# Sums of squares along the rows of x on ScalarE for groups two to eight, with a rewritten order of the preparation steps

## The chip, the core and the metric

The kernel runs on one core of a Trainium2 chip. The core has five engines with instruction queues of their own: TensorE (PE in the profile, its weight loads PEld), VectorE (DVE), ScalarE (ACT), GpSimd (POOL) and SyncE (SP, which here only issues transfers). Each works through its own instructions in program order and waits on semaphores for the others. Transfers run on 16 DMA engines. The metric is device time in microseconds (us) of one execution; of several executions the median counts.

## The reference: one hybrid attention and retention layer

The input is x (2048 tokens by 1024, float32), 256 context tokens `ctx`, a conditioning vector c with its twin `c_ctx`, and the weights of one layer. The part that matters here is the beginning: each token is normalised by its root mean square, scaled and shifted by vectors that come from c through the matrix `w_ada`, and projected by `w_in`.

```python
def _rmsnorm(x, g):
    xf = x.astype(jnp.float32)
    xf = xf * lax.rsqrt(jnp.mean(xf * xf, axis=-1, keepdims=True) + EPS)
    return (xf * g.astype(jnp.float32)).astype(x.dtype)
...
mod = jax.nn.silu(c) @ w_ada[i] + b_ada[i]
mod_c = jax.nn.silu(c_ctx) @ w_ada[i] + b_ada[i]
...
h_lat = _rmsnorm(x, norm_g[i]) * (1.0 + scale) + shift
h_ctx = _rmsnorm(ctx, norm_g[i]) * (1.0 + scale_c) + shift_c
...
y_lat, y_ctx = _mixer(h_lat, h_ctx, w_in[i], ...)
x = x + gate * y_lat
return _rmsnorm(x, final_norm_g)
```

`_mixer` projects h to eight blocks of columns, runs neighbourhood attention on four of them and two-way retention on the other four, and projects the result back. All of that stays as it is.

## The kernel before

**Groups.** The 2304 tokens are handled as nine groups of 256: groups 0 to 7 are x, group 8 is the context. The first stage makes h for each group and, while doing so, already projects it: block b (0 to 4) holds groups 2b and 2b+1, and `window(b)` runs 32 steps of three matmuls for it (four result tiles, `units`, of eight steps each). Products are made in pieces of a high and a low part, so h and the weights exist as `hi` and `lo` tiles. A step of block b has the number 32b + n, and `PLAN` names after which step each piece of preparation is issued. It is a table written out by hand; `run_acts` takes its entries in order. No scheduler changes it: what stands earlier in the program stands earlier in the queue of its engine.

**The pieces for group i.**
- `x`: the transposed group (features on partitions, tokens along the row) is loaded from `xT` (`load_x`, L182).
- `sq`: its squares and their partial sums over features (`squares`, L194). ScalarE squares two halves, and POOL and DVE add up the pieces into one 128x256 tile.
- `cs`: four small matmuls against a column of ones add over the partitions (`colsum`, L205), so that PSUM holds one sum per token.
- `rs`: DVE scales it and adds epsilon (L214), POOL raises it to the power -1/2 (L215), DVE copies it along a row (L220).
- `sp`: a matmul against the identity (`spread`, L222) turns it round, so that the factors lie along the row in PSUM.
- `mu`: DVE multiplies the group by the factors, half u at a time (L241).
- `ab`: scale and shift (`prep_ab`, L267), part on DVE, part on ScalarE; for groups 0 and 1 `p` does this per block of 128 features k together with the split into hi and lo (`prep_first`, L255).
- `hl`: ScalarE writes the hi part (L279), and POOL or DVE the lo part (L283).

**The vectors of c.** They come from four rows u of `w_ada`: `s` splits a piece, `m` multiplies (L311), `ar` copies the row out of PSUM (`ada_row`, L316), `af` turns it round and adds the bias (`ada_fin`, L321). Features k = 2u and 2u+1 need row u.

**What else runs there.** Every finished unit is evicted by `u_k` (L380): ScalarE casts it to the hi part (L383), DVE takes the lo part (L384), and SP stores both to `kS` in DRAM. The tile `o` for this has two buffers, so the third eviction waits until the first store has landed. `spill_step` (L249) stores h to `hS` in DRAM, one half group at every second step. The tiles named `st` (four of 512 KB) hold two groups of weights at first, then the squares, at last the context and weights again.

**Queues.** All loads and these stores are issued on SP in program order; an SP instruction that waits for data holds back every later one. `LOADS` is the list that SP issues first.

Of the kernel before, what the change touches and what calls it, by code (L numbers as in the profile page):

```python
# [9 lines left out]
F32 = mybir.dt.float32  # L10
BF16 = mybir.dt.bfloat16
F32R = mybir.dt.float32r
AF = mybir.ActivationFunctionType
# [5 lines left out]
P = 128  # L19
# [19 lines left out]
PLAN = [  # L39
# [19 lines left out]
]  # L59
SPL = [9, 0, 1, 0]  # L60
ALO = [0, 5, 9, 4]
# [21 lines left out]
def hybrid_kernel(ctx: ExitStack, tc: tile.TileContext, a: dict, out: bass.AP):  # L83
    nc = tc.nc
# [45 lines left out]
    KH = KC // 2  # L130
    env = dict(pp=pool(psx, "pp", 6, space=PSUM), st=pool(sx, "st", 4, side="right"), queue=nc.sync)

    def ptile(p=None):
        return (p or env["pp"]).tile([P, 512], F32, name="mm")
# [56 lines left out]

    sqs, rms, rbs, prs = {}, {}, {}, {}

    def squares(i):  # L194
        sqs[i] = []
        for u in range(2):
            sq = xsq[i][u] if i < 2 else env["st"].tile([P, KH, 256], F32, name="st")
            nc.scalar.activation(sq, raw[i][u], AF.Square)
            eng = (nc.gpsimd, nc.vector)[u]
            eng.tensor_tensor(sq[:, 0:2, :], sq[:, 0:2, :], sq[:, 2:4, :], ALU.add)  # L200
            eng.tensor_tensor(sq[:, 0, :], sq[:, 0, :], sq[:, 1, :], ALU.add)
            sqs[i].append(sq)
        nc.vector.tensor_tensor(sqs[i][0][:, 0, :], sqs[i][0][:, 0, :], sqs[i][1][:, 0, :], ALU.add)

    def colsum(*ii):  # L205
        pm = ptile(None if ii[0] < 4 else psm)
        for j, i in enumerate(ii):
            for t in range(2):
                nc.tensor.matmul(pm[:, 2 * j + t:2 * j + t + 1], sqs[i][0][:, 0, t * P:(t + 1) * P], one, start=True, stop=True)
            rms[i] = pm[:, 2 * j:2 * j + 2]  # L210

    def rstd(i):
        r = env["st"].tile([P, 2], F32, name="rs", bufs=4)
        nc.vector.tensor_scalar(r, rms[i], 1.0 / D, EPS, ALU.mult, ALU.add)  # L214
        nc.gpsimd.tensor_tensor(r, r, mhalf[:, 0:2], ALU.pow)  # L215
        rbs[i] = r

    def spread_copy(i):
        rbs[i, 1] = env["st"].tile([P, 2, P], F32, name="t0", bufs=2)
        nc.vector.tensor_copy(rbs[i, 1], rbs[i].unsqueeze(2).to_broadcast([P, 2, P]))  # L220
# [95 lines left out]
    def ada_row(u):  # L316
        rows[u] = op.tile([P, 2, 512], F32, name="o")[:, 0, :]
        n = 4 if SPL[u] else 2
        (nc.scalar.copy, nc.vector.tensor_copy)[u % 2](rows[u][0:n, :], aps[u][0:n, :])

    def ada_fin(u):  # L321
        pm, n = ptile(psm), 4 if SPL[u] else 2
# [141 lines left out]
    lds = dict(a=ada_load, x=load_x, c=small, w=lambda g: wr.append(w_raw(512 + 256 * g)))  # L464
    for name, *args in LOADS:
        lds[name](*args)
    acts = dict(sq=squares, cs=lambda *i: colsum(*i), rs=lambda i: (rstd(i), spread_copy(i)), sp=lambda *i: spread(*i),
                mu=lambda i, u: spread_mul(i, (u,)), ab=prep_ab, hl=prep_hl, blk=alloc_blk, x=load_x, w=lambda: wr.append(w_raw(2560)),
                w2=lambda: load_w(), s=ada_split, m=ada_mm, ar=ada_row, af=ada_fin, p=prep_first,
                ws=lambda g: w01.append(w_split(wr[g], lo=WSL[g])))  # L470
# [1151 lines left out]
```

## Time and profile before

| | |
|---|---|
| median of 3 runs | 1360.26 us (1356.26, 1360.26, 1361.77) |
| profiled execution, its own time | 1357.68 us |
| its span, from the first to the last instruction | 1355.7 us |
| mean granted TensorE clock | 0.996 |
| matmul instructions in the profile | 8236 |
| bytes moved by DMA | 287.25 MB |

Times inside the kernel are counted from the start of the span. A row of the timeline gives start, duration, engine, line, operation, written and read tiles, shape, a count and, in brackets, the idle time of the engine before it and what ended it. Durations of consecutive matmuls overlap, so the pace of TensorE is read from the distance of their starts. The stage that this document is about takes the first 165 us or so.

### The profile page before, as it was taken

To read this page: it belongs to the slowest core of one execution; us is meant where nothing else is said; L and a number is where in the kernel's file an instruction comes from. 1 tells how busy PE (TensorE), PEld (TensorE's weight loads), DVE (VectorE), ACT (ScalarE), POOL (GpSimd) and SP (SyncE) were. 2 spreads that over 40 slices of the span, in tenths; PEclk is the share of its full clock that TensorE was granted. 3 is DMA by queue.
4 is the path that set the end of the run, shared out by engine and by line. 5 is a ranking of instruction groups with operands and counts; after the bars stand their busy time and mean duration, and the time that the engine had idled before them with its cause. 6 is when DMAs were issued, how large, how long until landed. Compare 5 with 4: busy or idle time off the path is not lost.

```text
span 1355.7 us, 23094 instructions
## 1 busy us (share of the span) xinstructions
PE 1310.1 (97%) x8236; PEld 1146.9 (85%) x8236; DVE 828.3 (61%) x1444; ACT 606.5 (45%) x1259; POOL 579.9 (43%) x569
## 2 busy tenths in 40 slices
PE   6999999999999999999999999999999899999997
PEld 2477899887897788998999889889999789888886
DVE  5687366676766755377767777776654633445345
ACT  4454343343533344455555465556643244333432
POOL 4443101554034664445535474655523154544442
PEclk9999999999999999999999999999999999999999
DMA  9386788464867656978587886666528888555433
GB/s 363 135 279 231 259 313 215 164 210 147 326 182 230 216 203 213 265 210 211 148 225 207 226 224 206 195 181 193 163 90 291 278 290 279 159 163 171 163 121 129
DMA packets 172085, 287.25 MB, mean 212 GB/s; under 512 B 17345, under 2 KB 92225, under 8 KB 170690
## 3 DMA queue, kind: packets, MB, share of 16 engines
q1 hardware_dynamic: 139554, 228.35, 55.8%
q10 hardware_dynamic: 32416, 57.42, 11.8%
q8 instruction: 66, 1.08, 0.3%
q14 instruction: 49, 0.40, 0.1%
HBM read 194.48 MB, written 91.23 MB: 211 GB/s over the span
## 4 chain that ended last, share of the span: by engine, by line
PE 70%; DVE 9%; DMA 8%; POOL 4%; issue 4%; ACT 3%; SPq 1%; ACTq 0%; DVEq 0%; POOLq 0%
PE mm L374 17%; PE mm L671 12%; PE mm L1463 11%; PE mm L363 7%; PE sS L1025 4%; PE tr L1052 3%; PE po L1073 3%; PE mm L1187 2%; PE mm L311 2%; PE tr L1054 2%; PE po L1075 2%; DMA v<-rvS 1%; PE mm L1375 1%; POOL hlo L531 1%; PE mm L1374 1%
## 5 line engine op out<-in xcount | busy, mean ns | idle before, releaser
L374 PE MATMUL mm<-whi,hlo 128*128 128x256 f32 x832 | 228.6, 282 | 1.0 <-DMA hlo<-cS 1.0
L374 PE MATMUL mm<-whi,hhi 128*128 128x256 f32 x768 | 224.3, 292 | 0.0
L374 PE MATMUL mm<-wlo,hhi 128*128 128x256 f32 x768 | 216.8, 282 | 0.0
L1056 ACT CAST pt<-tr 128x640 fp32r<-128x640 f32 (+1 forms) x128 | 95.6, 747 | 160.4 <-PE tr L1054 157.8
L1062 DVE TENSOR_TENSOR pt<-tr,pt 128x640 fp32r<-128x640 f32 (+1 forms) x128 | 114.0, 890 | 78.4 <-ACT pt L1056 77.2
L374 PEld LDWEIGHTS mm<-whi,hlo 128*128 128x128 f32 x832 | 156.6, 191 | 1.4 <-DMA hlo<-cS 1.3
L1045 POOL TENSOR_SCALAR sp<-sp,stt 128x640 f32<-128x640 f32 (+2 forms) x128 | 103.1, 808 | 106.3 <-DVE stt L1044 75.7
L374 PEld LDWEIGHTS mm<-whi,hhi 128*128 128x128 f32 x768 | 146.3, 191 | 0.0
L374 PEld LDWEIGHTS mm<-wlo,hhi 128*128 128x128 f32 x768 | 146.1, 190 | 0.0
L1034 DVE CUSTOM_DVE_ANT_0 sp<-sS,nb 128x640 f32<-128x640 f32 (+2 forms) x128 | 105.6, 825 | 33.4 <-DMA nb<-in_rpb_t_dram 20.7
L1039 ACT ACTIVATE sp<-sp,stt 128x640 f32<-128x640 f32 (+2 forms) x128 | 107.4, 839 | 20.3 <-DVE stt L1034 19.1
L625 POOL TENSOR_TENSOR whi<-st,whi 128x512 fp32r<-128x512 f32 x48 | 62.8, 1330 | 107.7 <-ACT whi L624 107.7
L363 PE MATMUL mm<-hhi,whi 128*128 128x512 f32 x256 | 108.2, 423 | 0.0
L363 PE MATMUL mm<-hlo,whi 128*128 128x512 f32 x256 | 102.0, 399 | 6.0 <-DVE hlo L265 2.1
L1025 PE MATMUL sS<-k,q 128*128 128x256 f32 (+3 forms) x512 | 99.1, 315 | 5.1 <-DVE stt L1034 4.7
L363 PE MATMUL mm<-hhi,wlo 128*128 128x512 f32 x256 | 102.0, 398 | 0.3 <-DVE wlo L347 0.3
L671 PE MATMUL mm<-hhi,whi 128*128 128x512 f32 x336 | 98.1, 395 | 1.6 <-POOL whi L625 1.6
L1463 PE MATMUL mm<-wor,y 128*128 128x512 f32 x384 | 95.7, 398 | 1.1 <-DVE xt L1472 1.1
L1472 DVE TENSOR_TENSOR xt<-mm,xt 128x512 f32<-128x512 f32 x64 | 43.9, 687 | 82.6 <-PE mm L1463 82.5
L1025 PEld LDWEIGHTS sS<-k,q 128*128 128x128 f32 x512 | 82.8, 188 | 12.0 <-DVE stt L1034 8.2
L1463 PE MATMUL mm<-won,y 128*128 128x512 f32 x336 | 89.9, 406 | 0.0
L625 POOL TENSOR_TENSOR wlo<-st,wlo 128x512 fp32r<-128x512 f32 x36 | 53.1, 1476 | 75.8 <-ACT wlo L624 73.7
(258 smaller groups left out, 3051.5 us busy)
## 6 DMA issues: line engine op xcount, KB each, us to landing
st<-in_w_in_dram SPq DMA_DIRECT2D x64, 512.0 KB
q<-qS SPq DMA_DIRECT2D x64, 256.0 KB
hlo<-hS SPq DMA_DIRECT2D x20, 512.0 KB
k<-kS SPq DMA_DIRECT2D x16, 576.0 KB
kS<-o SPq DMA_DIRECT2D x16, 512.0 KB
vB<-o SPq DMA_DIRECT2D x64, 128.0 KB
qS<-o ACTq DMA_DIRECT2D x16, 512.0 KB
woS<-g ACTq DMA_DIRECT2D x32, 256.0 KB
```

Source lines behind the costliest of these rows:

```text
L363: nc.tensor.matmul(pm[:, :n], ww[:, k, cs], h[:, k, :], start=(k == 0 and i == 0), stop=(k == KC - 1 and i == 2))
L374: nc.tensor.matmul(pm[:, t * WG:(t + 1) * WG], h[:, k, o:o + P], ww[:, k, :], start=(k == 0 and i == 0), stop=(k == KC - 1 and i == 2))
L625: nc.gpsimd.tensor_tensor(t[:, 1], r, f(t)[:, 0], ALU.subtract)
L671: nc.tensor.matmul(pm, ww[:, k, :], hh[:, k, :], start=(k == 0 and i == 0), stop=(k == KH - 1 and i == 2))
L1025: nc.tensor.matmul(o, hd["q"][i][:, hl, j * P:(j + 1) * P], k, start=(hl == 0), stop=(hl == 1))
L1034: nc.vector.tensor_tensor_reduce(T["sp"][:, :n], T["s"], nbz[big][:, o:o + n], -1.0, 3e38, ALU.add, ALU.min, T["st"][:, 0:1])
L1039: nc.scalar.activation(sp[:, :n], sp[:, :n], AF.Exp, bias=st[:, 0:1], scale=-1.0, accum_out=st[:, 1:2])
L1045: nc.gpsimd.tensor_scalar(sp[:, :n], sp[:, :n], st[:, 2:3], 0.0, ALU.mult, ALU.add)
L1056: nc.scalar.copy(pt[:, :ng_ + 2, 0, :], tr[:, :ng_ + 2, :])
L1062: nc.vector.tensor_tensor(pt[:, :n, 1, :], tr[:, :n, :], f(pt)[:, :n, 0, :], ALU.subtract)
L1463: nc.tensor.matmul(pm, yy[:, k, :], ww[:, k, sl], start=(k == 0 and i == 0), stop=(k == 3 and i == 2))
L1472: nc.vector.tensor_tensor(xts[t][:, sl], pm, xts[t][:, sl], ALU.add)
```

## The change

Groups 2 to 8 no longer get their sums from the transposed group. A new piece `xt` (`load_xt_`) loads the same group from x itself (or `ctx`), tokens on partitions, as two tiles of 128x1024, into the `st` buffers. `squares` for these groups is then two ScalarE instructions that square a tile in place and add up along its row; the sum goes straight to an SBUF tile of one value per token. The additions on POOL and DVE, the matmuls of `colsum` and the read from PSUM are gone for them. Groups 0 and 1 are left as they were. `ada_row` copies the third row (u = 2) with DVE instead of ScalarE. `PLAN` is rewritten: in particular group five is squared together with group four, the `sp` of groups 2 and 3, 4 and 5 come two steps earlier, and the context is loaded at step 46 instead of 79.

```diff
-    (12, 'p', 5), (12, 'm', 3, 1), (12, 'p', 4), (13, 'sq', 4), (13, 'cs', 2, 3), (13, 'm', 3, 2), (14, 'm', 3, 3),
+    (13, 'm', 3, 2), (13, 'm', 3, 3), (14, 'sp', 2, 3), (14, 'mu', 2, 0), (14, 'mu', 3, 0), (14, 'sq', 4), (14, 'sq', 5),
...
+    def load_xt_(i):
+        sqs[i] = []
+        src = a["ctx"] if i == 8 else a["x"][i * 256:(i + 1) * 256, :]
+        for t in range(2):
+            xt = env["st"].tile([P, KH, 256], F32, name="st").rearrange("p k t -> p (k t)")
+            nc.sync.dma_start(xt, src[t * P:(t + 1) * P, :])
+            sqs[i].append(xt)
+
     def squares(i):
+        if i >= 2:
+            rms[i] = env["st"].tile([P, 2], F32, name="rs", bufs=4)
+            for t, xt in enumerate(sqs[i]):
+                nc.scalar.activation(xt, xt, AF.Square, accum_out=rms[i][:, t:t + 1])
+            return
         sqs[i] = []
         for u in range(2):
-            sq = xsq[i][u] if i < 2 else env["st"].tile([P, KH, 256], F32, name="st")
+            sq = xsq[i][u]
...
-        pm = ptile(None if ii[0] < 4 else psm)
+        pm = ptile()
...
-        r = env["st"].tile([P, 2], F32, name="rs", bufs=4)
+        r = rms[i] if i >= 2 else env["st"].tile([P, 2], F32, name="rs", bufs=4)
...
-        (nc.scalar.copy, nc.vector.tensor_copy)[u % 2](rows[u][0:n, :], aps[u][0:n, :])
+        (nc.scalar.copy, nc.vector.tensor_copy)[u > 0](rows[u][0:n, :], aps[u][0:n, :])
```

The lines behind the new code stand 13 lines later than in the kernel before (L383 becomes L396, and so on). Three places show how the order of instructions moves.

The first is DVE in block 0, where the spread factors of groups 2 and 3 are made and row 3 is copied. Before, L214 and L220 are a group's `rs`, L319 the copy of row 3, L329 and L332 its `af`, L241 the first `mu` of group 2:

```order
L214 TENSOR_SCALAR rs<-mm 128x2
L220 COPY t_447<-rs 128x256
L319 COPY o<-mm 2x512
L214 TENSOR_SCALAR rs<-mm 128x2
L220 COPY t_457<-rs 128x256
L329 TENSOR_TENSOR mods<-mm,bada 128x8
L332 SCALAR_TENSOR_TENSOR mods<-mods,ng 128x4
L241 TENSOR_TENSOR hlo<-hlo,mm 128x1024
```

The same place after the change, where L254 is `mu`, L285 `ab`, L332 the copy of row 3, L342 and L345 its `af`:

```order
L227 TENSOR_SCALAR rs<-rs 128x2
L233 COPY t_429<-rs 128x256
L254 TENSOR_TENSOR hlo<-hlo,mm 128x1024 x2
L285 TENSOR_SCALAR hlo<-hlo,mods 128x256 x4
L332 COPY o<-mm 2x512
L254 TENSOR_TENSOR hlo<-hlo,mm 128x1024
L342 TENSOR_TENSOR mods<-mm,bada 128x8
L345 SCALAR_TENSOR_TENSOR mods<-mods,ng 128x4
```

The copy of row 3 now stands behind two `mu` and four scalings that wait for the spread. On TensorE the spread of groups 2 and 3 stands two steps ahead of the turning of row 3; before, it stood right behind it.

The second is the passage from block 0 to block 1. On ScalarE before, L279 is a hi part, L383 the cast of an eviction, L198 the squares of groups 5 and 6, L274 a scaling:

```order
L279 CAST hhi<-hlo 128x4x256 x2
L383 CAST o<-mm 128x512
L198 ACTIVATE st<-hhi 128x1024 x2
L383 CAST o<-mm 128x512
L274 ACTIVATE hhi<-hhi,mods 128x256 x2
L383 CAST o<-mm 128x512 x2
L274 ACTIVATE hhi<-hhi,mods 128x256 x2
L198 ACTIVATE st<-chi 128x1024 x2
```

After the change, where L206 is the squares of groups 6 and 7:

```order
L292 CAST hhi<-hlo 128x4x256 x2
L396 CAST o<-mm 128x512 x3
L206 ACTIVATE st,rs<-st 128x1024 x2
L396 CAST o<-mm 128x512
L287 ACTIVATE hhi<-hhi,mods 128x256 x2
L206 ACTIVATE st,rs<-st 128x1024 x2
L396 CAST o<-mm 128x512
```

All four evictions of block 0 stand behind the hi parts of groups 2 and 3, where the first two stood ahead of or between them; the squares of group 7 stand between the fourth and the fifth eviction. On SP before, from the first `kS` store on (`chi` is the load of group 6):

```order
L151 DMA kS_62<-o 256x1x512
L253 DMA hS_87<-hhi 128x4x256
L190 DMA chi<-in_xT_dram 128x1024 x2
L151 DMA kS_63<-o 256x1x512
L253 DMA hS_87<-hhi 128x4x256
L151 DMA kS_64<-o 256x1x512
```

And after the change:

```order
L151 DMA kS_62<-o 256x1x512
L266 DMA hS_87<-hhi 128x4x256
L190 DMA chi<-in_xT_dram 128x1024 x2
L266 DMA hS_87<-hhi 128x4x256
L151 DMA kS_63<-o 256x1x512
L266 DMA hS_87<-hhi 128x4x256
L151 DMA kS_64<-o 256x1x512
```

One more store of h stands ahead of the second `kS` store.

The third is the end of block 1. On ScalarE before, L279 is the hi part of group 5's second half, L198 the squares of group 7:

```order
L274 ACTIVATE hhi<-hhi,mods 128x256
L383 CAST o<-mm 128x512
L279 CAST hhi<-hhi 128x4x256
L383 CAST o<-mm 128x512
L198 ACTIVATE st<-clo 128x1024 x2
```

After the change, where L206 is the squares of group 8:

```order
L287 ACTIVATE hhi<-hhi,mods 128x256
L396 CAST o<-mm 128x512
L206 ACTIVATE st,rs<-st 128x1024 x2
L292 CAST hhi<-hhi 128x4x256
L396 CAST o<-mm 128x512 x2
```

The squares of group 8 stand ahead of that hi part. What they read is loaded by SP among the stores of block 1, from the fourth `kS` store on:

```order
L151 DMA kS_61<-o 256x1x512
L266 DMA hS_88<-hlo 128x4x256 x3
L151 DMA kS_61<-o 256x1x512
L176 DMA st<-in_ctxT_dram 128x1024 x2
L151 DMA kS_62<-o 256x1x512
L199 DMA st<-in_ctx_dram 128x1024 x2
L190 DMA clo<-in_xT_dram 128x1024 x2
```

Before, only `clo`, the load of group 7, stood there (L190, behind the sixth `kS` store), and the context followed behind the ninth.

More of the change, by code (lines that the diff above doesn't have):

```diff
@@ L466, in hybrid_kernel @@
         lds[name](*args)
-    acts = dict(sq=squares, cs=lambda *i: colsum(*i), rs=lambda i: (rstd(i), spread_copy(i)), sp=lambda *i: spread(*i),
+    acts = dict(sq=squares, xt=load_xt_, cs=lambda *i: colsum(*i), rs=lambda i: (rstd(i), spread_copy(i)), sp=lambda *i: spread(*i),
                 mu=lambda i, u: spread_mul(i, (u,)), ab=prep_ab, hl=prep_hl, blk=alloc_blk, x=load_x, w=lambda: wr.append(w_raw(2560)),
```

32 rows, old and new, of the table PLAN are left out of this document.

## The prediction, made before the result

> **What bounds the kernel now.** I read the page first, then TensorE's waits, then the timeline of each engine up to 165 us.
>
> ```profile
> PE 1310.1 (97%) x8236; PEld 1146.9 (85%) x8236; DVE 828.3 (61%) x1444; ACT 606.5 (45%) x1259; POOL 579.9 (43%) x569
> 180.00:200.00 20.00, 20.00 (x169) 20.00 (x169) 11.37 (x11) 7.71 (x10) 0.00 (x0) 1.00 0.96 337
> ```
>
> The second row is a stretch of the windows (length, busy time of the five engines, granted clock, DMA share, GB/s). TensorE bounds the kernel; from about 165 us on it hardly waits, so what the change wins or loses in the first stage should reach the end undiminished. TensorE's waits up to 300 us, but for 10.2 us at the very start that the change leaves alone:
>
> ```profile
> PE mm L363 <- DVE hlo L265: 2.1, 2, 1.7
> PE mm L363 <- DVE hlo L283: 2.0, 1, 2.0
> PE mm L227 <- DVE t L220: 1.5, 1, 1.5
> PE mm L363 <- POOL hlo L283: 1.4, 1, 1.4
> ```
>
> These, with the column sums themselves, are what there is to win. In TensorE's timeline they lie here:
>
> ```profile
> 38.46 0.50 PE L363 MATMUL mm<-hlo,whi 128*128 128x512 f32 x1 [1.73 <-DVE hlo L265]
> 39.13 3.00 PE L311 MATMUL mm<-hlo,silc 128*2 128x512 f32 x4
> 53.92 0.95 PE L209 MATMUL mm<-one,st 128*128 128x1 f32 x8
> 54.79 1.88 PE L311 MATMUL mm<-clo,silc 128*2 128x512 f32 x4
> 59.30 0.51 PE L363 MATMUL mm<-hhi,whi 128*128 128x512 f32 x1
> 61.24 1.33 PE L227 MATMUL mm<-ident,t 128*128 128x128 f32 x8
> 62.32 0.48 PE L363 MATMUL mm<-hhi,whi 128*128 128x512 f32 x1
> 76.55 0.47 PE L363 MATMUL mm<-hlo,whi 128*128 128x512 f32 x1 [1.96 <-DVE hlo L283]
> 82.09 0.39 PE L363 MATMUL mm<-hhi,whi 128*128 128x512 f32 x1
> ...
> 85.04 0.39 PE L363 MATMUL mm<-hlo,whi 128*128 128x512 f32 x1
> 85.50 0.50 PE L209 MATMUL mm<-one,st 128*128 128x1 f32 x4
> 85.86 0.47 PE L363 MATMUL mm<-hhi,whi 128*128 128x512 f32 x1
> 91.43 0.60 PE L227 MATMUL mm<-ident,t 128*128 128x128 f32 x4
> 103.04 0.50 PE L363 MATMUL mm<-hlo,whi 128*128 128x512 f32 x1 [1.45 <-POOL hlo L283]
> 108.47 0.71 PE L227 MATMUL mm<-ident,t 128*128 128x128 f32 x4 [1.51 <-DVE t L220]
> 78.00:80.00 2.00, 2.00 (x6) 1.52 (x6) 2.00 (x2) 1.09 (x2) 2.00 (x2) 0.50 0.93 258
> ```
>
> From 82.09 to 85.04 are 13 starts, 0.227 us each: a step of three matmuls takes 0.68 us. The last row shows the clock granted after the wait at 76.55: 0.50. Eight matmuls come 0.43 apart there, so that wait cost a further 8 x 0.2 = 1.6.
>
> **The change part by part.**
>
> *Column sums.* The four matmuls of groups 2 and 3 take 54.79 - 53.92 = 0.87, the two of one group 85.86 - 85.50 = 0.36. With groups 4 to 8 that is 0.87 + 5 x 0.36 = 2.7 us of TensorE time.
>
> *Additions.* DVE and POOL lose them. The wait at 38.46 goes back to these rows:
>
> ```profile
> 34.35 0.40 DVE L263 TENSOR_SCALAR hhi<-hhi,mods 128x256 f32<-128x256 f32 x1
> 36.11 1.37 DVE L263 TENSOR_SCALAR hhi<-hhi,mods 128x256 f32<-128x256 f32 x1
> 37.52 0.90 DVE L265 TENSOR_TENSOR hlo<-hhi 128x256 fp32r<-128x256 f32 x1
> 35.87 1.46 POOL L200 TENSOR_TENSOR st<-st 128x512 f32<-128x512 f32 x1
> ```
>
> The same scaling takes 0.40 alone and 1.37 while POOL adds squares. Without them the lo part comes 0.97 + 0.47 = 1.44 earlier (0.43 is its time alone). The slow stretch behind the wait (3.00 for four where 54.79 shows 1.88, and 0.6 in the next step) should go with it: 0 to 1.7. I take 1.7, since a wait of 0.3 is left.
>
> *Loads.* 7.3 MB of rows are added. The first loads end at 45 us and leave the DMA engines idle until 72:
>
> ```profile
> 40.00:45.00 5.00, 5.00 (x10) 1.30 (x9) 2.59 (x4) 0.00 (x0) 0.82 (x1) 0.68 1.00 397
> 45.00:50.00 5.00, 5.00 (x19) 2.27 (x18) 0.28 (x2) 2.48 (x3) 1.26 (x1) 1.00 0.04 14
> ```
>
> The rows of groups 2 and 3 take the place of groups 4 and 5 in that queue and land by 45; the rest lands by 60 and costs nothing.
>
> *Squares.* No row shows the new form, but the end of the kernel has a ScalarE square with a sum: the same square plus a read of the accumulator.
>
> ```profile
> L1419 ACT ACTIVATION_READ_ACCUMULATOR ot<-xt x32: 185/187/224, 1160.8 to 1349.9; 128x1 f32 x32
> L198 ACT ACTIVATE st<-hlo x4: 1042/1042/1054, 34.3 to 48.6; 128x1024 f32<-128x1024 f32 x4
> ```
>
> So a group costs 2 x (1.04 + 0.19) = 2.46 on ScalarE. Groups 2 and 3 are done by 47.5, ahead of row 2's scalings, which need that row about then.
>
> *Block 0.* The spread of groups 2 and 3 stood at 61.24, behind two steps and row 3's turning (61.24 - 59.30 = 1.94) which now follow it. So it starts at 59.3 - 0.87 - 1.44 - 1.7 = 55.3. But row 3's copy now stands on DVE behind two `mu` and four scalings that wait for it:
>
> ```profile
> 59.95 0.67 DVE L319 COPY o<-mm 2x512 f32<-2x512 f32 x1
> 62.60 1.22 DVE L241 TENSOR_TENSOR hlo<-hlo,mm 128x1024 f32<-128x1024 f32 x1 [0.53 <-PE mm L227]
> 69.31 0.72 DVE L272 TENSOR_SCALAR hlo<-hlo,mods 128x256 f32<-128x256 f32 x2
> ```
>
> DVE begins 62.60 - 61.24 = 1.36 behind the spread, then 2.4 + 1.4 + 0.67: the copy ends at 61.1. TensorE, done with its two steps at 55.3 + 1.1 + 1.4 = 57.8, waits **3.3**. It goes on at 61.5 (62.32 before), loses 1.6 to the clock, and then needs nothing that is late but the factors of group 4 (0.5): block 0 ends at 61.5 + 15 x 0.68 + 1.6 + 0.4 + 0.5 = 74.2, as before. Its 4 us are given back.
>
> *Start of block 1.* On DVE from 61.1: `mu` 1.2, row 3 0.4, then ScalarE's four scalings and hi part 3.1, then DVE's lo part 1.2, `mu` 1.1, scalings 1.4, factors of group 4 1.3, ScalarE 1.0, lo part 1.2: 73.0. All h of groups 2 and 3 is there at 73.0, so the 1.96 and 1.6 at 76.55 go, and block 1 runs **3.6** ahead.
>
> *The spread of group 5.* DVE makes its factors behind the fifth eviction:
>
> ```profile
> 72.48 0.63 SPq L151 DMA_DIRECT2D kS<-o  x1
> 83.09 0.59 ACT L383 CAST o<-mm 128x512 fp32r<-128x512 f32 x1 [4.00 <-DMA kS<-o]
> 86.74 0.59 ACT L383 CAST o<-mm 128x512 fp32r<-128x512 f32 x1 [2.07 <-DMA kS<-o]
> 87.36 0.69 DVE L384 TENSOR_TENSOR o<-mm,o 128x512 fp32r<-128x512 f32 x1 [1.18 <-ACT o L383]
> 87.97 0.15 DVE L214 TENSOR_SCALAR rs<-mm 128x2 f32<-128x2 f32 x1
> 88.94 0.29 DVE L220 COPY t<-rs 128x256 f32<-128x256 f32 x1 [0.82 <-POOL rs L215]
> 90.00:92.00 2.00, 2.00 (x13) 1.73 (x12) 1.34 (x3) 2.00 (x4) 0.00 (x0) 1.00 1.06 359
> ```
>
> The fourth cast waits for the second `kS` store, 83.09 - 72.48 = 10.6 behind the first one's issue. Now the first store is issued at 73.0 + 0.7 + 0.2 = 73.9, and one more hS store (0.52 MB at 359 GB/s, 1.5) lies ahead of the second: the fourth cast comes at 86.0. Behind it on ScalarE stand two scalings (1.1) and group 7's squares (2.46), then the fifth cast (0.6): 90.7. DVE 0.7 and the factors 1.27 (87.97 to 89.23) give 92.7. TensorE is there at 74.2 + 17 x 0.68 = 85.8, two steps earlier in the program, and waits **7**. If the store landed at 83.1 as before, it would wait 4. Before, TensorE stood at the same step at 91.43 - 1.36 = 90.1. So it is now 92.7 - 90.1 = 2.6 behind, and 1.6 for the clock makes **+4.2**.
>
> The Trainium skill, page "TensorE: Matmul & The Clock Gate", section "What's actually happening", says that the clock halves after an idle window of about 3.4 us. The trace shows it halved after a wait of 1.96, so here the measurement decides; an estimate by that page would give 1.7 for the wait of 7 and leave the 3.3 of block 0 perhaps unpunished, and the sum would be the same, as block 0's end has 0.5 of waiting left to absorb it.
>
> *Block 2.* The waits 1.45 and 1.51 and the column sums of groups 6 to 8 (3 x 0.36) go, since DVE has no additions between `mu` and `ab` of group 5: **-4.0**. New is that group 5's last hi part stands behind group 8's squares on ScalarE. Their rows are issued behind the sixth kS store. From the fourth store (87.2) on, 5.24 MB lie ahead of their end (ten transfers of 0.52), 14.6 us at 359 GB/s: 102 to 105. Then 1.23 + 1.05 + 1.21 for half the squares, hi and lo part: 105.5 to 108.5, where TensorE comes at 92.7 + 0.4 + 19 x 0.68 + 1.6 = 107.6; the factors of group 6 stand 1.27 behind. A wait of 0 to 1.5; I take **+0.7**.
>
> *Sum.* +4.2 - 4.0 + 0.7 = **+0.9**. The later blocks have the additions taken off and nothing put on. The profiled execution took 1357.68, 2.6 under the median of the runs shown; on that median 0.9 gives about 1361.
>
> **The rivals.**
>
> *The stores aren't late* (the fifth eviction is done before TensorE needs group 5's factors): the whole 90.1 - 85.8 = 4.3 at that step stays, and with the 4.0 of block 2 the kernel gains 8.3: 1352. For it speaks that no run shows the new queue; against it, the two DMA waits of ScalarE above, in the very same buffers. Chance 0.22.
>
> *They land as before, at 83.1*: 2.9 less, and no wait in block 2, 0.7 less: 1357. Chance 0.2.
>
> *Slower*: the rows of group 8 come late. If the queue drains at the 258 GB/s of the row 78.00:80.00 instead of 359, 5.24 MB take 20.3 us, the lo part comes at 111 to 114 in place of 105.5 to 108.5, and TensorE waits 3.4 to 6.6 in block 2 in place of the 0.7, with a further 1.6 for the clock: +5 to +8, 1365 to 1369. It decides as soon as the rows land later than 104.1 (107.6 - 3.5). For it: hS stores go out in short rows, and 253 to 258 were seen while they ran; against it, 359 to 399 in the rest of that stretch. Chance 0.16.
>
> *The change doesn't do what it says*: if ScalarE's squares were no cheaper in the end than the additions they replace, 2.46 for 2.08 on ScalarE would still be off the path everywhere but ahead of the fifth cast; that is inside the sum.
>
> **How the numbers follow.** Forecast 1361, chance 0.42, from 1358 to 1364. The range takes in the first rival at its low end and half of the slower one: 1351 to 1367. A measurement of this kernel tells about 0.5%, 6.8 us, from no change. Faster by more than that: the first rival, 0.22. Slower: the upper part of the slow one, 0.1. Within: 0.68.
>
> **What would show it.** In the profile after: a wait of L337 for DVE's copy of row 3 near 58 us; no wait where block 1 begins; a wait of L240 for DVE's factors (L233) near 86 us, with ScalarE's L396 waiting for `kS` stores before it; and a wait of a matmul for group 5's lo part near 107, with ScalarE's L206 waiting for `in_ctx_dram`. If L240 near 86 us doesn't wait, the first rival is right. If the first of these waits leaves TensorE behind 74.2 at the end of block 0, the gain of block 1 is smaller still. Were the time outside the range, I would look first for a wait behind 165 us, where I expect none that is new.

## The result, and the profile after

The changed kernel took 1368.76 us (median of 6 runs, 1366.23 to 1372.13), the kernel before 1360.40 beside it (6 runs): a ratio of 1.0070, 95% interval 1.0052 to 1.0089. It is slower by 8.4 us. Its profiled execution took 1366.32 us with a span of 1364.5, which is 8.8 more than the span before. Of all executions below one, of rows_only, took 4559.56 us and is left out of that kernel's ratio.

TensorE's waits up to 300 us after the change (us in total, times, longest):

```profile
PE mm L240 <- DVE t L233: 10.9, 3, 9.0
...
PE mm L337 <- DVE o L332: 3.0, 1, 3.0
PE mm L376 <- DVE hlo L278: 2.6, 2, 2.3
PE mm L387 <- ACT whi L358: 2.4, 1, 2.4
PE mm L387 <- DVE wlo L360: 0.8, 1, 0.8
PE mm L376 <- DVE hlo L296: 0.6, 1, 0.6
```

The waits of the kernel before for lo parts (2.0 and 1.4 us) and for the factors of group 6 (1.5 us) are gone or small, and larger ones have come. Where they lie in TensorE's timeline:

```profile
60.01 0.38 PE L337 MATMUL mm<-ident,o 2*128 2x2 f32 x4 [3.03 <-DVE o L332]
...
67.24 0.47 PE L376 MATMUL mm<-hlo,whi 128*128 128x512 f32 x1 [2.27 <-DVE hlo L278]
...
71.31 0.71 PE L240 MATMUL mm<-ident,t 128*128 128x128 f32 x4 [1.33 <-DVE t L233]
...
96.06 1.20 PE L240 MATMUL mm<-ident,t 128*128 128x128 f32 x4 [9.05 <-DVE t L233]
...
112.34 0.50 PE L376 MATMUL mm<-hlo,whi 128*128 128x512 f32 x1 [0.60 <-DVE hlo L296]
...
176.19 0.39 PE L387 MATMUL mm<-whi,chi 128*128 128x256 f32 x1 [2.38 <-ACT whi L358]
...
177.45 0.39 PE L387 MATMUL mm<-wlo,chi 128*128 128x256 f32 x1 [0.76 <-DVE wlo L360]
```

To see when the time is lost, the same two instructions are read in both traces: DVE's lo part of the last eviction of block 3, and the first of the later evictions that DVE makes behind the context. Before:

```profile
153.86 0.69 DVE L384 TENSOR_TENSOR o<-mm,o 128x512 fp32r<-128x512 f32 x1 [4.93 <-ACT o L383]
...
201.05 0.69 DVE L413 TENSOR_TENSOR o<-mm,o 128x512 fp32r<-128x512 f32 x1
```

And after:

```profile
157.32 0.69 DVE L397 TENSOR_TENSOR o<-mm,o 128x512 fp32r<-128x512 f32 x1 [4.93 <-ACT o L396]
...
209.37 0.69 DVE L426 TENSOR_TENSOR o<-mm,o 128x512 fp32r<-128x512 f32 x1
```

The changed kernel is 3.5 us behind at the end of block 3, and 8.3 behind 50 us later. From there to the end it is mostly 6.6 to 9.3 behind. So there are two losses, **3.5 us in blocks 0 to 3** and **4.8 us around the context**.

*The first loss.* DVE and POOL of the changed kernel where block 0 ends:

```profile
62.34 3.89 DVE L276 TENSOR_SCALAR hhi<-hhi,mods 128x256 f32<-128x256 f32 x4 [1.07 <-ACT hhi L275]
...
69.29 0.72 DVE L285 TENSOR_SCALAR hlo<-hlo,mods 128x256 f32<-128x256 f32 x2
...
71.17 2.87 DVE L285 TENSOR_SCALAR hlo<-hlo,mods 128x256 f32<-128x256 f32 x2
61.88 2.41 POOL L296 TENSOR_TENSOR hlo<-hlo,hhi 128x1024 fp32r<-128x1024 f32 x1 [8.68 <-ACT hhi L292]
64.52 2.29 POOL L278 TENSOR_TENSOR hlo<-hhi 128x256 fp32r<-128x256 f32 x3 [0.23 <-DVE hhi L276]
...
71.50 2.39 POOL L296 TENSOR_TENSOR hlo<-hlo,hhi 128x1024 fp32r<-128x1024 f32 x1 [0.57 <-ACT hhi L292]
```

Two scalings take 0.72 us alone and 2.87 beside a lo part on POOL, and they end at 74.04, right behind that lo part's end at 73.89. The four of L276 take 3.89, where two pairs alone would take 1.44. All evictions of block 0 stand behind these. What follows from that, on SP, ScalarE and DVE:

```profile
77.06 0.63 SPq L151 DMA_DIRECT2D kS<-o  x1
89.83 0.58 ACT L396 CAST o<-mm 128x512 fp32r<-128x512 f32 x1 [6.06 <-DMA kS<-o]
95.62 0.29 DVE L233 COPY t<-rs 128x256 f32<-128x256 f32 x1 [0.88 <-POOL rs L228]
```

The first `kS` store is issued at 77.06, the fourth cast waits for the second store until 89.83, and the factors of group 5, which stand behind the fifth cast, are there at 95.9.

*The second loss.* ScalarE casts the context's four units of 256 columns to `o` and issues their stores itself; behind the second and the fourth cast stand the casts of the next weights (`whi`). Before:

```profile
156.95 0.61 ACTq L151 DMA_DIRECT2D kS<-o  x1
...
160.00 0.52 ACTq L151 DMA_DIRECT2D kS<-o  x1
...
165.83 0.37 ACT L383 CAST o<-mm 128x256 fp32r<-128x256 f32 x1 [3.27 <-DMA kS<-o]
...
167.31 0.37 ACT L383 CAST o<-mm 128x256 fp32r<-128x256 f32 x1 [1.11 <-DVE o L384]
...
168.73 2.00 ACT L345 CAST whi<-st 128x1024 fp32r<-128x1024 f32 x2 [1.05 <-DVE o L384]
```

After:

```profile
160.41 0.58 ACTq L151 DMA_DIRECT2D kS<-o  x1
...
163.25 0.52 ACTq L151 DMA_DIRECT2D kS<-o  x1
...
170.45 0.37 ACT L396 CAST o<-mm 128x256 fp32r<-128x256 f32 x1 [4.64 <-DMA kS<-o]
...
173.67 0.37 ACT L396 CAST o<-mm 128x256 fp32r<-128x256 f32 x1 [2.85 <-DMA kS<-o]
...
175.09 1.99 ACT L358 CAST whi<-st 128x1024 fp32r<-128x1024 f32 x2 [1.05 <-DVE o L397]
```

The first two stores go out 3.3 to 3.5 us later, as all else does there. But the first lands 10.0 us behind its issue in place of 8.9, and the second 10.4, where before it took no more than 7.3 and nobody waited for it. The casts of the weights come 6.4 us late, and TensorE waits 2.38 and 0.76 us, where it waited 0.5 before, and then runs at a lower clock: 0.82 and 0.84 in the two stretches of 5 us from 175 to 185, which is 1.7 us of lost time. Together that is 4.3 of the 4.8.

Why they land later shows in part in the transfers. These are the 4 us behind the issue of the first store, in the kernel before and in the changed one (the last two numbers are the busy share of the DMA engines and GB/s):

```profile
156.95:160.95 4.00, 4.00 (x36) 4.00 (x35) 0.42 (x1) 0.76 (x2) 0.00 (x0) 1.00 0.94 308
...
160.41:164.41 4.00, 4.00 (x36) 4.00 (x35) 0.42 (x1) 0.97 (x2) 0.00 (x0) 1.00 0.95 226
```

The DMA engines are as busy but move a quarter less.

### The profile page after: what moved, and what is told of

The parts are those of the page before. It is cut to its first block, busy times and chain, and to the rows that moved or that the text cites. A ratio compares the mean times of both kernels' runs of the same rounds, so it can differ in the third digit from the quotient of the medians.

```text
span 1364.5 us, 23028 instructions
## 1 busy us (share of the span) xinstructions
PE 1306.4 (96%) x8208; PEld 1146.6 (84%) x8208; DVE 818.3 (60%) x1424; ACT 607.3 (45%) x1272; POOL 563.1 (41%) x555
## 4 chain that ended last, share of the span: by engine, by line
PE 68%; DMA 12%; DVE 6%; ACT 4%; POOL 4%; issue 3%; SPq 2%; ACTq 0%; DVEq 0%; POOLq 0%
PE mm L387 17%; PE mm L684 15%; PE mm L1476 11%; PE mm L376 6%; PE sS L1038 4%; PE tr L1065 3%; PE po L1086 3%; PE mm L1200 2%; PE tr L1067 2%; PE po L1088 2%; DMA st<-in_x_dram 2%; DMA kS<-o 1%; DMA st<-in_w_in_dram 1%; DMA v<-rvS 1%; POOL hlo L544 1%
## 5 line engine op out<-in xcount | busy, mean ns | idle before, releaser
L1047 DVE CUSTOM_DVE_ANT_0 sp<-sS,nb 128x640 f32<-128x640 f32 (+2 forms) x128 | 105.5, 824 | 34.2 <-PE sS L1038 28.2
L1038 PEld LDWEIGHTS sS<-k,q 128*128 128x128 f32 x512 | 82.8, 188 | 12.1 <-DVE stt L1047 8.4
L1476 PEld LDWEIGHTS mm<-wor,y 128*128 128x128 f32 x384 | 69.9, 188 | 17.6 <-issue 3.5
```

The lines of the kernel that those rows point to most:

```text
L1038: nc.tensor.matmul(o, hd["q"][i][:, hl, j * P:(j + 1) * P], k, start=(hl == 0), stop=(hl == 1))
L1047: nc.vector.tensor_tensor_reduce(T["sp"][:, :n], T["s"], nbz[big][:, o:o + n], -1.0, 3e38, ALU.add, ALU.min, T["st"][:, 0:1])
L1476: nc.tensor.matmul(pm, yy[:, k, :], ww[:, k, sl], start=(k == 0 and i == 0), stop=(k == 3 and i == 2))
```

## The experiments

The theory: two separate losses, both waits for `kS` stores. In block 1 the first stores go out late, since DVE's scalings run beside POOL and all evictions of block 0 stand behind them; around the context the stores land later. The rivals: the row-wise sums themselves cost what they save; the place of one piece (the copy of row 3, the factors of group 5) is the loss; or the 4.8 us are a chance of one execution.

"At 154" and "at 201" are read from each kernel's trace at the two instructions shown above, less 153.86 and 201.05: us behind the kernel before (minus: ahead). Ratios are to the kernel before, with 95% intervals; a kernel that ran once has none.

| kernel | median us (runs) | ratio | at 154 | at 201 |
|---|---|---|---|---|
| changed | 1368.76 (6) | 1.0070 (1.0052 to 1.0089) | 3.5 | 8.3 |
| repeat | 1366.62 (1) | | 3.1 | 6.9 |
| rs5_early | 1374.01 (4) | 1.0102 (1.0069 to 1.0135) | 5.8 | 10.2 |
| row3_first | 1367.60 (6) | 1.0065 (1.0041 to 1.0090) | 3.5 | 8.2 |
| rows_only | 1359.50 (10) | 1.0000 (0.9982 to 1.0018) | -0.6 | 1.8 |
| ctx_pairs | 1365.34 (9) | 1.0046 (1.0029 to 1.0063) | 3.5 | 3.5 |
| lo_dve | 1366.25 (1) | | 5.3 | 7.3 |
| rows_pairs | 1359.09 (10) | 1.0002 (0.9987 to 1.0016) | 0.2 | -0.6 |
| reordered | 1359.74 (10) | 1.0000 (0.9986 to 1.0015) | 0.7 | 0.4 |
| evict_first | 1365.33 (10) | 1.0044 (1.0026 to 1.0062) | -1.0 | 6.2 |
| before_pairs | 1358.12 (10) | 0.9992 (0.9976 to 1.0007) | -0.1 | 0.3 |
| reordered2 | 1354.91 (12) | 0.9968 (0.9954 to 0.9982) | -4.3 | -3.3 |
| evict_pairs | 1360.24 (12) | 1.0002 (0.9985 to 1.0019) | -1.2 | -0.8 |

Behind 201 us a single trace drifts by up to 5 us against another (`ctx_pairs` was 5.9 behind at 1004 us and 8.9 at its end, evict_first 3.4 and 4.8), so single profiles are compared up to there only. One source of it is the clock: in seven of the fourteen traces, the kernel before not among them, it was halved for 3.4 us or more near 450 us.

**repeat**, the changed kernel again.

> The changed kernel, unaltered. Its profile shows TensorE 3.5 us behind the kernel before at 126 to 160 us and 8 us behind from 201 us on; the step between them comes with ScalarE waiting 4.64 and 2.85 us at 170 to 174 us for the context's kS stores, where the kernel before waits 3.27 and then not for a store. Theory A (a lasting effect of the new order: the stores meet the reloads of h at a worse moment): the same two waits, 4.6 and 2.9 within 0.7 us, and TensorE 7.5 to 8.5 us behind at 201 us. Theory B (a chance of one execution, transfers that happened to run slowly): the second wait is gone or under 1 us and TensorE stays 3 to 4 us behind at 201 us, so a span of 1360 to 1361 us.

TensorE's 9.05 us came again as 9.0, its 3.0 came again too, and around the context 2.2 and 0.8. ScalarE's two waits there were 5.08 and 2.27. The second loss was 3.8 us, not 4.8, a little under what theory A said (6.9 behind at 201, not 7.5), and far from the 3 to 4 behind of theory B: it is no chance of one execution.

**rows_only**, the old order with the new sums.

```diff
-    (13, 'sq', 4), (13, 'cs', 2, 3), ...
+    (13, 'xt', 4), (13, 'sq', 4), ...
```

> The order of the kernel before, with only the row-wise sums of squares put in (the loads of x for them placed 1 to 45 us ahead of use; row 3's copy on DVE as both kernels have it, row 2's on ScalarE as before). The theory (the loss comes from the rewritten order, the row-wise sums themselves take work away): the waits 1.73 at 38 us, 1.45 and 1.51 at 103 to 108 us shrink or go with the additions, none of 2 us or more is added, and the time is 1350 to 1357, faster than the kernel before by 3 to 10 us. The rival (the added loads and the longer squares on ScalarE cost what the additions cost, whatever the order): 1359 to 1366.

No difference from the kernel before: the rival's time. The additions' waits went (1.73 at 38 us), but half a dozen of 1.0 to 1.5 us came, mostly for hi and lo parts. So the row-wise sums gain nothing in the old order, but the 8 us do not come from them.

**row3_first**

```diff
-    (14, 'sp', 2, 3), (14, 'mu', 2, 0), ... (15, 'ar', 3),
+    (14, 'sp', 2, 3), (14, 'ar', 3), (14, 'mu', 2, 0), ...
```

> The changed kernel with the copy of row 3 on DVE ahead of the two multiplications and four scalings of groups 2 and 3, where DVE idles from 53.5 to 55.6 us. The theory (that wait only covers a later one: the last four features of groups 0 and 1 wait for ScalarE, which is busy with groups 2 and 3 until 61.7 us, and for scalings on DVE that take 3.89 us beside POOL): the wait of L337, 3.03 us, is gone, and the wait of the following matmul for hlo (2.27 us at 67.24 us) grows to 5 to 5.5 us; block 0 ends where it did within 0.5 us and the time is 1366 to 1372. The rival (the place of row 3's copy is what block 0 loses by): the second wait stays at 2.3 us, block 0 ends 3 us earlier, and the time falls by 3 us or more.

```profile
63.72 0.51 PE L376 MATMUL mm<-hhi,whi 128*128 128x512 f32 x1 [1.48 <-ACT hhi L275]
67.07 0.77 PE L376 MATMUL mm<-hlo,whi 128*128 128x512 f32 x1 [2.84 <-DVE hlo L278]
```

The wait of L337 is gone, and the next waits have grown to 1.48 and 2.84, 4.32 together in place of 2.27 (5 to 5.5 expected). Behind them the clock was halved for 3.4 us, which it was not in the changed kernel. Block 0 ends where it did, and about so without that: the spread of group 4, a few steps on, needs factors that DVE has at 71.1 here and at 71.25 in the changed kernel. The 3.03 us had covered the next waits.

**lo_dve**

```diff
-LOV = {..., 2: 0, ...}
+LOV = {..., 2: 1, ...}
```

> The changed kernel with the lo part of group 2's first half on DVE in place of POOL. The theory (DVE's scalings take 3.89 us for four instead of 1.46 because they run beside POOL's 2.41 us lo part): the four scalings near 62 us take 1.4 to 2.4 us, DVE gets a lo part of 1.2 us ahead of them, and the lo parts that TensorE waits for at 67.24 us are there 0 to 1 us earlier. The rival (they take long for another reason, such as ScalarE's pace on the same tiles): 3.5 us or more as before. The time is 1364 to 1368 either way.

```profile
65.69 2.44 DVE L276 TENSOR_SCALAR hhi<-hhi,mods 128x256 f32<-128x256 f32 x4 [0.67 <-ACT hhi L275]
63.77 0.55 PE L337 MATMUL mm<-ident,o 2*128 2x2 f32 x4 [6.70 <-DVE o L332]
```

With one POOL instruction taken from beside them the four scalings fell from 3.89 to 2.44 us, the theory's upper end (POOL's L278 still runs beside them). But the lo part now held up DVE's copy of row 3, which stands behind it and which I had overlooked: TensorE waited 6.70 us at L337 in place of 3.03, and the kernel was 5.3 us behind at 154.

**rs5_early**

```diff
-    (19, 'rs', 4), ... (40, 'rs', 5),
+    (19, 'rs', 4), (19, 'rs', 5), ...
```

> The changed kernel with the factors of group 5 made right behind those of group 4 (near 71 us), ahead of all evictions on DVE. The theory (TensorE's 9.05 us at the spread of group 5 are a matter of DVE's order, but group 5's first multiplication still stands behind the sixth eviction, and its last hi part behind group 8's squares): the wait of L240 near 96 us is gone, TensorE passes that spread at 87 us, then waits up to 2 us at step 56 for a PSUM buffer and 8 to 11 us more for the lo parts of group 5 in block 2, so that the start of block 3 moves by less than 2 us; time 1366 to 1371. The rival (that wait is the loss): 9 to 10 us are gained and 1358 to 1360 us come out.

```profile
102.01 0.80 PE L376 MATMUL mm<-hhi,whi 128*128 128x512 f32 x1 [4.57 <-ACT hhi L292]
106.46 0.79 PE L376 MATMUL mm<-hlo,whi 128*128 128x512 f32 x1 [3.65 <-POOL hlo L296]
```

The wait at the spread is gone and comes back in block 2 as 4.57 and 3.65 us for the hi and lo parts of group 5, as the theory said; with two stretches at half clock there (100.7 to 110.9 and 114.4 to 117.8 us) the kernel is 2.3 us worse at 154, and its time, 1374 us, lies above the 1366 to 1371 expected. The factors are only the first thing behind the late stores.

**evict_first**

```diff
-    (20, 'ab', 3, 1), (21, 'hl', 2, 1), (22, 'hl', 3, 1),
+    (25, 'ab', 3, 1), (25, 'hl', 2, 1), (25, 'hl', 3, 1),
```

> The changed kernel, with the last scalings and hi parts of groups 2 and 3 issued behind the first eviction of block 0 instead of ahead of it. The theory (TensorE's wait at the spread of group 5 is set by when the first two kS stores are issued): the first kS store is issued at 69 to 72 us in place of 77.06, the third cast doesn't wait for a store, the fourth cast comes at 85.5 to 88 in place of 89.83, and the wait of L240 near 96 us falls from 9.05 to 5 to 7.5 us; block 1 may start up to 1 us later. The time is 1365 to 1368. The rival (the second store's landing hangs on the stores of h and the loads around it, not on the first eviction): the fourth cast stays at 89 to 90 and the wait at 8.5 to 9.5 us.

On SP, ScalarE (twice), TensorE, and ScalarE at the context:

```profile
72.11 0.63 SPq L151 DMA_DIRECT2D kS<-o  x1
...
85.46 0.59 ACT L396 CAST o<-mm 128x512 fp32r<-128x512 f32 x1 [6.48 <-DMA kS<-o]
...
91.70 1.19 PE L240 MATMUL mm<-ident,t 128*128 128x128 f32 x4 [4.45 <-DVE t L233]
...
166.10 0.37 ACT L396 CAST o<-mm 128x256 fp32r<-128x256 f32 x1 [4.70 <-DMA kS<-o]
...
169.11 0.37 ACT L396 CAST o<-mm 128x256 fp32r<-128x256 f32 x1 [2.64 <-DMA kS<-o]
```

One eviction moved ahead brings the first store to 72.11, the fourth cast to 85.46 and TensorE's wait from 9.05 to 4.45. The first loss turns into a gain of 1.0 at 154. The second loss is all there, although this kernel isn't late when it gets to the context: it doesn't come from the lateness. It is 7.2 us here and not 4.8, mainly because the clock behind it was halved for 6.8 us in place of 3.4; TensorE's waits, 2.2 and 0.8, are nearly the same.

**ctx_pairs**

```diff
+        if b == 4 and ct == 1:
+            o, s = half[0], slice(n, 2 * n)
+        else:
+            o = half[0] = op.tile([P, 2, 512], F32R, name="o")
```

> The changed kernel, with the four evictions of the context (256 columns each) put in pairs into one tile o, so that the third and fourth need no landing of the first two stores. The theory (from 160 to 201 us the changed kernel loses another 4 to 5 us because ScalarE waits 4.64 and 2.85 us for these landings, and the casts of the next weights stand behind them): both waits and TensorE's waits for whi and wlo at 175 to 178 us (2.4 and 0.8) go, TensorE stays 3.5 us behind the kernel before at 201 us in place of 8, and the time is 1361 to 1364. The rival (the weights' own loads are late by then, so the casts wait for them instead): less than 1.5 us of it is gained, 1365 to 1369.

ScalarE at the context:

```profile
165.80 0.36 ACT L402 CAST o<-mm 128x256 fp32r<-128x256 f32 x1
...
168.27 0.37 ACT L402 CAST o<-mm 128x256 fp32r<-128x256 f32 x1 [2.10 <-PE mm L376]
...
171.22 2.00 ACT L358 CAST whi<-st 128x1024 fp32r<-128x1024 f32 x2 [2.58 <-DMA kS<-o]
```

The third and fourth cast no longer wait for stores. By its row the cast of the weights still stands 2.58 us behind a landing, but it comes 3.9 us earlier than in the changed kernel, TensorE waits for neither `whi` nor `wlo`, and the kernel is 3.5 us behind at 201 as it is at 154. So up to 201 us the second loss is those waits and the slow clock behind them. The time fell by less: 1365.34 us lies where the rival had put it. The step from 1.0070 to 1.0046 is 3.3 us, with intervals that overlap, and by itself doesn't settle it; evict_pairs does.

**before_pairs** and **rows_pairs**, the same edit in the kernel before and in rows_only.

> A control: the kernel before, with the context's evictions in pairs. There ScalarE waits 3.27 us for a store at 165.83 us, but TensorE only 0.5 us for the weights behind it. The theory (what the pairs won in the changed kernel is a loss that the new order had brought): no measurable difference, 1357.5 to 1360, TensorE 0.3 to 1 us ahead at 201 us. The rival (the pairs help any version, so that the loss belongs to both kernels): 1354 to 1357.

> The kernel with the old order and the row-wise sums, with the context's evictions in pairs as well. That kernel was 0.7 us ahead of the kernel before at 160 us and 1.8 us behind at 201 us. The theory (the same late landings): it stays 0.5 to 1 us ahead at 201 us, and the time is 1355 to 1358. The rival (the loss there has another source): no change, 1358 to 1361.

The kernel before gains nothing that can be measured, and at 201 it is 0.3 us behind, not ahead as expected: there the waits were covered. rows_only fell back by 2.3 us between 154 and 201, and with the pairs it no longer does (0.2 behind, then 0.6 ahead). Its time, 1359.09, is the rival's: no measurable fall.

**evict_pairs**, both edits.

> The changed kernel with two edits together: the first eviction ahead of the last hi parts of groups 2 and 3, and the context's evictions in pairs. Alone, the first left TensorE 1.0 us ahead of the kernel before at 160 us but 6.2 behind at 201 us; the second 3.5 behind at both. The theory (these two are the whole of the loss, and they add): 0.5 to 1.5 us ahead at 201 us, and the time is 1357 to 1361, no longer different from the kernel before. The rival (a third loss stands behind them, later or in the pairs' own stores): still 3 us or more behind at 201 us or at 560 us, 1362 to 1366.

1.2 us ahead at 154, 0.8 ahead at 201, and no difference from the kernel before. Both were expected. The two edits undo the whole loss.

**reordered** and **reordered2**, the changed kernel with a new `PLAN`. The first has row 3 ahead, then the last features of groups 0 and 1, group 5 multiplied ahead of the fourth eviction, and the edit of ctx_pairs. The second has all that, the edit of evict_first, groups 4 and 5 split earlier, and (entries in the order in which they are issued):

```diff
-LOV = {0: 2, 1: 2, 2: 0, 3: 3, 4: 2, 5: 2, ...}
+LOV = {0: 2, 1: 2, 2: 3, 3: 3, 4: 3, 5: 3, ...}
...
+    (14, 'ar', 3), (14, 'sp', 2, 3), (14, 'sq', 4), (14, 'rs', 4), (14, 'mu', 2, 0), (14, 'mu', 3, 0), (14, 'sq', 5),
+    (14, 'blk', 1), (15, 'af', 3), (15, 'mu', 2, 1), (15, 'xt', 6), (16, 'p', 7), (16, 'p', 6), (16, 'xt', 7),
+    (18, 'ab', 2, 0), (18, 'ab', 3, 0), (18, 'rs', 5), (18, 'hl', 2, 0), (18, 'hl', 3, 0), (19, 'mu', 3, 1),
+    (25, 'ab', 2, 1), (25, 'ab', 3, 1), (25, 'hl', 2, 1), (25, 'hl', 3, 1), (26, 'sp', 4), (26, 'x', 6),
+    (28, 'mu', 4, 0), (29, 'sp', 5), (30, 'mu', 4, 1), (31, 'mu', 5, 0), (31, 'mu', 5, 1), (31, 'ab', 4, 0),
+    (33, 'sq', 6), (34, 'ab', 4, 1), (36, 'ab', 5, 0), (36, 'ab', 5, 1), (46, 'x', 8), (49, 'blk', 2),
+    (50, 'xt', 8), (50, 'hl', 4, 0), (50, 'hl', 5, 0), (50, 'hl', 4, 1), (51, 'hl', 5, 1), (53, 'x', 7),
+    (55, 'blk', 3), (56, 'sq', 7), (62, 'sq', 8), ...
```

> The changed kernel with the faults that the runs have shown taken out together: row 3 copied and turned first, the last features of groups 0 and 1 ahead of the scalings of groups 2 and 3, the factors of groups 4 and 5 made as soon as their squares are there, group 5 multiplied ahead of the fourth eviction, the squares of group 7 behind the fifth eviction and those of group 8 behind group 5's last hi part, group 2's lo parts on DVE, the context's evictions in pairs. The theory (each of these waits is a matter of order): no wait of TensorE over 3 us between 50 and 130 us, block 1 starts at 69 to 73 us in place of 75.5, and the time is 1349 to 1356. The rival (the kS stores pace block 1 and 2 whatever stands where): TensorE waits 5 us or more between 75 and 115 us for PSUM or lo parts, 1357 to 1364.

> The reordered kernel, further: the second halves of groups 2 and 3 behind the first eviction, the factors of group 5 ahead of group 2's lo parts, all lo parts of groups 2 to 5 on DVE, groups 4 and 5 split at step 50 instead of 55, squares of group 7 behind that. It waited 1.13, 1.28, 2.61, 0.60, 3.37 and 1.97 us between 60 and 130 us. The theory (all of these are order and DVE beside POOL): the 2.61 us for an eviction and the 3.37 us for POOL's lo part go, the 1.28 us for the factors of group 5 too; TensorE is 3 to 6 us ahead of the kernel before at 160 us and the time is 1353 to 1357. The rival (the stores or the transfers of h, which come no earlier, take what is won): 1358 to 1361.

reordered missed its 1349 to 1356 and only got level with the kernel before: waits of 3.37 us for a lo part on POOL and 2.61 for a late eviction stood in it. reordered2 came out as its theory said and is faster than both kernels, 0.9968 (0.9954 to 0.9982) of the kernel before. Its remaining waits for factors are those of groups 6 and 7:

```profile
PE mm L240 <- DVE t L233: 6.7, 2, 4.3
```

On DVE both stand behind an eviction. The first eviction's cast waits for a store until 96.04, though the squares of group 6 are done by 85.7; the second's stands on ScalarE behind the squares of group 8, which wait for their rows until 102.2 and 105.0.

## Why the prediction was wrong

- **Right: the copy of row 3 and the start of block 1.** I wrote a wait of 3.3 us near 58 us; it was 3.03. Block 1 began without a wait.
- **Wrong: block 0 then "needs nothing that is late but the factors of group 4 (0.5)".** It waited 2.27 us for lo parts of groups 0 and 1, and 1.33 for the factors. The 1.6 for the clock that I had added there didn't come in this execution; in repeat it did, and the 2.27 was 0.61. TensorE came to the spread of group 5 at 96.06 - 9.05 = 87.0, not 85.8.
- **Wrong, the step that failed in the first stage: the chain on DVE "from 61.1 ... 73.0".** I added the durations of lone instructions, although POOL's lo parts of the same groups run beside them. The four scalings of L276 and the lo part behind them had no term, and alone they would just have been hidden beside ScalarE's 3.1 (2.3 from 62.34 on, against 64.7); they kept DVE until 67.0. Of the term of 1.4 for the four scalings of groups 2 and 3, half took 0.72 as priced and half 2.87. The two cost 2.3 and 2.2 us; the chain had been 1.1 early. The profile before had the price in it. I had read the same effect off it at 0.40 against 1.37 and used it only to credit its removal; and it had these four scalings beside POOL's lo part of 71.74 to 74.15:

```profile
72.36 2.90 DVE L272 TENSOR_SCALAR hlo<-hlo,mods 128x256 f32<-128x256 f32 x4
```

The first store was issued at 77.06 in place of 73.9, and what hangs on it came about as predicted from there: the fourth cast 12.8 us later (12.1 predicted), the factors at 95.9 (92.7 plus the same 3.2; the chain behind the fourth cast was 0.6 shorter than predicted, which evens this out). So the wait was 9.05, not 7. lo_dve shows the effect of POOL on the four of L276, evict_first that the first stores set the wait; no run takes POOL from beside all six scalings and leaves the rest alone. Not tested either is how far ScalarE shares in it: its squares of groups 4 and 5 waited 2.69 us for rows until 56.47, ahead of the hi part that lets POOL's first lo part start, although the loads were to "cost nothing".
- **Right, in part by luck: block 2.** I wrote -4.0 + 0.7, and the new waits were 0.60 and 0.52. But the squares of group 8 began at 107.7, not at 102 to 105, and the lo part came at 112.3, not at 105.5 to 108.5. TensorE was 4 us late as well (111.7 in place of 107.6), since both hang on the late first store, and so the wait stayed small. Of the predicted +0.9 at this place 3.5 came out; the 2.6 between are the late spread (96.06 against 92.7, 3.4) less 0.8 that I can't place.
- **Wrong, the larger part: "from about 165 us on it hardly waits", so that what the first stage does "should reach the end undiminished"; "nothing put on" for the later blocks.** 4.8 us were added there. The profile before did show ScalarE waiting 3.27 us for a store with the weights' casts behind it, and TensorE 0.5 us for `wlo`: the cover was thin, and I didn't price it. The prediction did name a wait behind 165 us as the first place to look. ctx_pairs, evict_first and before_pairs show cause and place.
- **The rivals.** The stores were late (fourth cast at 89.83), so neither rival with stores in time holds. The slower one had a time near the result (1365 to 1369) and 0.16, and its sign came: the rows of group 8 landed later than 104.1. But its mechanism didn't make the loss, since TensorE, late itself, waited only 0.60 for what stands behind them.

Open: what in the new order makes the context's stores land later. It isn't the lateness of the stage (evict_first). In all eight traces of the changed kernel and of its edits other than reordered and reordered2, the DMA engines moved 212 to 232 GB/s in the 4 us behind the first store's issue, and 292 to 308 in the six of the kernel before, rows_only, these two with pairs, reordered and reordered2. Where the stores are not in pairs, the first landed 9.8 to 10.5 us behind its issue in the former, and 8.7 and 8.9 in the kernel before and rows_only. So the late landing goes with this `PLAN`, and not with the row-wise sums alone; by the GB/s, other new orders don't have it. What the transfers meet there was not tried. rows_only's own 2.3 us are another matter: its stores land as before (8.7 and 7.4), and TensorE waits 1.6 us for weights in place of 0.5.

## What to carry to other kernels

Before adding up durations on an engine, look at what runs beside each on the other engines: the price of an instruction that is moved is the price at its new place. A wait that is removed is worth what it uncovers; two edits here removed waits of 3 and 9 us and gained nothing, while moving the first store of a chain ahead by 5 us gained 4.5 at the end of the stage. And a stage counts as safe from a change upstream only if its own near misses (an engine that waits for a landing with a critical cast behind it) have slack.

## What the hardware showed

**DVE beside POOL.** In rs5_early a small copy that takes 0.29 us alone met a lo part on POOL:

```profile
71.97 2.48 DVE L233 COPY t<-rs 128x256 f32<-128x256 f32 x1 [0.88 <-POOL rs L228]
71.90 2.39 POOL L296 TENSOR_TENSOR hlo<-hlo,hhi 128x1024 fp32r<-128x1024 f32 x1
```

It ended at 74.45, 0.16 behind POOL's instruction at 74.29, as the pair of scalings in the changed kernel ended 0.15 behind POOL's (74.04 and 73.89). That fits an instruction that is held until POOL is done better than one that is slowed throughout. The Trainium skill, page "SBUF — State Buffer", section "Who interferes with whom", says that DVE's copies and scalings can run in a fast form that needs the pair of ports which GpSimd uses too, under an exclusive lock, and that the later one is fully blocked until the first is done. The trace agrees, and by that rule the scalings of the first loss could have been priced beforehand at what is left of POOL's instruction beside them.

**The clock.** A wait's length alone doesn't tell whether the clock falls. These are windows of the changed kernel behind its wait of 3.03 us, of repeat behind the same wait of 3.02, and of the changed kernel behind its waits of 2.38 and 0.76 (the granted clock is the third number from the end of a row):

```profile
57.00:62.00 5.00, 1.99 (x11) 1.73 (x12) 4.24 (x9) 4.87 (x10) 0.12 (x1) 1.00 0.77 237
...
62.00:64.00 2.00, 2.00 (x6) 1.54 (x6) 1.85 (x1) 2.00 (x5) 2.00 (x1) 0.50 0.92 329
...
175.00:180.00 5.00, 3.05 (x16) 2.85 (x17) 3.81 (x4) 4.37 (x5) 0.00 (x0) 0.82 0.42 129
```

The same wait in the same program was followed by full clock in one execution and by half clock in the other. 2.38 and 0.76 us close together were followed by a slow stretch, and so was 1.96 in the kernel before. By the traces' records of the clock, every slow stretch inside these fourteen executions lasts 3.4, 6.8 or 10.2 us (77.3 to 80.7 in the kernel before, 172.2 to 179.0 in evict_first, 89.5 to 99.7 in the changed kernel, most of it in the wait of 9.05). So one trace can't price a wait to better than the 1.7 us that a stretch of 3.4 us at half clock costs.
